# New prices in the builder's account of time: products and powers in the first block, passages between engines in the second

## The chip, the cores and the metric

The kernel runs on one core of a Trainium2 chip. The metric is the device time of one execution in microseconds (us); the times are medians of several runs. The profile is of one execution, with the time of each instruction on each engine: TensorE (PE, with its weight loads PEld), VectorE (DVE), ScalarE (ACT), GpSimd (POOL) and SyncE (SP, which issues the loads).

## What is computed

A row of 256 tokens of width 1024 goes through two blocks, in float32. The first block has two layers. Each norms its input, multiplies it with `w_in`, and mixes the tokens in three ways: retention (6 heads), dilated causal attention (6 heads) and a gated mixing within chunks of 128 tokens. The result goes through `w_out`, is normed and added; then comes a hidden layer of 2816 units.

```
for l in range(DEPTH):
    x = hybrid_layer(x, cos, sin, g_mix_pre[l], g_mix_post[l], w_in[l], w_s[l], b_s[l], w_out[l],
                     g_ffn_pre[l], g_ffn_post[l], w_gate_up[l], w_down[l])
```

The second block has an even layer (a Fourier mixing and attention with compressed keys, over the tokens and over 256 further context tokens) and an odd one (attention in a window with 16 heads, and to the context). Both take shifts, scales and gates from a vector times `w_mod`, the modulation. At the end `x` is normed.

## The kernel before

**Products.** Every weight is loaded as float32 in pieces of up to 128 x 1024 and split into a high part `whi` (by ACT) and a low part `wlo` (by DVE, a few by POOL). The activations are split the same way, into `xh` and `xl`. A product is then three passes of TensorE: high by high, high by low, low by high (`mm3`, and `mmT` with the weights held still). Their results stand in PSUM tiles: `mm` for input and hidden products, `sc` for scores and the sums of the mixing output and of the hidden layer, `tr` (two of them) for transpositions, small products and the modulation, and in the second block `s` for scores and outputs of attention.

**Order of the work.** TensorE's instructions run in the order in which the builder writes them; on the other engines the tile framework orders the work, with priorities that the builder gives. So the builder decides what TensorE does while ACT and DVE work on a head. It keeps an account of time for that, the class `Flow`: `now` is TensorE's time, `chain` the time at which the task in hand has its last result. `mm` and `transpose` (lines 366 to 381) add the cost of an instruction to `now`. `Lane.call` gives each instruction of ACT, DVE and POOL a cost (`Lane.cost`, line 281) and books it on its engine's lane in `Flow.op` (line 143); the next step of the task can start a latency `LAT` later. `from_pe` starts a chain one latency after TensorE's last product.

The tasks are generators: `rope` heads to turn, `dilated_task`, `retain_task`, `gmlp_task`, `y_att_task`, `y_ret_task`, the `Edge` between two parts of a layer (a norm of the sums: `rpost` and `rpre` are powers -0.5 on POOL, then `yn` is transposed), `modnorm_task`, and in the second block `unit`, `values`, `pair` and `mixed` for the heads. Each yields where it has to wait. A heap holds it with the time at which the account says that it can go on; `pump` runs up to three that are due after each triple of the big products. Where the big products themselves must wait (`wait`, `until`), the tasks that come due are run, and in a gap of 0.6 us or more `fill_gap` runs a piece of the modulation.

The lines that decide this:

```
def op(self, lane, cost):
...
    self.chain = t + cost + LAT
...
def pump(self, n=3):
    c = self.chain
    while n and self.heap and self.heap[0][0] + MARGIN <= self.now:
        self.run(heapq.heappop(self.heap)[2])
        n -= 1
    self.chain = c
...
if self.name == "pool":
    return 0.06 + n * (0.3e-3 if op == "memset" else 2.0e-3)
```

**Modulation.** `mod_step` (line 873) takes one to three loaded tiles of `w_mod` and multiplies each with 32 columns of the vector in four products that lie beside each other in TensorE's columns, in plain float32 (two instructions each in the trace). `mod_until` calls it at fixed places, `mod_spare` in gaps; in all there are 48 tiles. The next tile is loaded on SP's queue, where the weight loads are too.

**Loads and splits.** `load_ahead` issues the next weight load when the account has a raw buffer free, `fill` splits what has come, up to 4 us ahead of `now`, into a ring of eight pairs of tiles in the first block and five in the second.

The first block ends at line 1574, where its pools are closed; then the second begins. In the profile the first block's mixing lies at about 30 to 190 and 360 to 525 us, its hidden layers at 195 to 355 and 525 to 700 us, the even layer at 700 to 960 and the odd one at 960 to 1125 us.

Of the kernel before, what the change touches and what calls it, by code (L numbers as in the profile page):

```python
# [12 lines left out]
F32R = mybir.dt.float32r  # L13
# [3 lines left out]
OP = mybir.AluOpType  # L17
# [94 lines left out]
class Ev:  # L112


    def __init__(self):
        self.t = None
        self.waiters = []


LAT = 0.22  # L120
TR = "tr"
GAP = 0.6
MARGIN = 0.0
# [2 lines left out]
class Flow:  # L126
# [5 lines left out]
    def __init__(self):  # L132
        self.now = 0.0
        self.chain = 0.0
        self.heap = []
        self.n = 0
        self.lanes = {}
        self.tr = [0.0, 0.0]
        self.mm = [0.0, 0.0]
        self.marks = []  # L140
        self.spare = None

    def op(self, lane, cost):
        busy = self.lanes.setdefault(lane, [])
        while busy and busy[0][1] < min(self.now, self.chain) - 20.0:
            busy.pop(0)
        t = self.chain
        i = 0
        for i, (s, e) in enumerate(busy):
            if s - t >= cost:  # L150
                break
            t = max(t, e)
        else:
            i = len(busy)
        busy.insert(i, (t, t + cost))
        self.chain = t + cost + LAT


    def mark(self):
# [80 lines left out]

    def from_pe(self):

        self.chain = self.now + LAT

    def take_mm(self):
        self.mm.sort()
# [13 lines left out]
class Lane:  # L260
# [22 lines left out]
    def cost(self, op, n, kw):  # L283
        if self.name == "act":
            c = 0.06 + n * 0.833e-3
            if kw.get("accum_out") is not None:
                c += 0.1
            return c + (0.13 if n > 16 and kw.get("bias") is not None else 0.0)
        if self.name == "pool":
            return 0.06 + n * (0.3e-3 if op == "memset" else 2.0e-3)  # L290
        if op == "tensor_copy":
            return 0.08 + n * 0.8e-3
        return 0.07 + n * 1.04e-3
# [32 lines left out]
def block_kernel(ctx: ExitStack, tc: tile.TileContext, A, out, stop=None):  # L326
    nc = tc.nc
    pe = nc.tensor
    F = Flow()
# [3 lines left out]
    def pool(name, bufs=1, stack=ctx, **kw):  # L333
        return stack.enter_context(tc.tile_pool(name=name, bufs=bufs, reuse_waits="tile", **kw))
# [21 lines left out]
    def mmtile():  # L356
        F.take_mm()
        return pm.tile([P, 512], F32, name="mm")

    def trtile(dt=F32):  # L360
        F.take_tr()
        return pt.tile([P, 512], dt, name="tr")
# [5 lines left out]
    def mm(o, lhsT, rhs, start, stop_, cost=None, **kw):  # L368
        n = 1
        for s in o.shape[1:]:  # L370
            n *= s
        pe.matmul(o, lhsT, rhs, start=start, stop=stop_, **kw)  # L372
        if cost is None:
            cost = max(0.107, n * 0.417e-3 + 0.003) if lhsT.dtype == F32R else 2 * max(0.107, n * 0.833e-3 + 0.003)
        F.now += cost
        F.chain = max(F.chain, F.now + LAT)

    def transpose(o, i, idt):
        pe.transpose(o, i, idt)  # L379
        F.now += 0.056 if i.dtype == F32R else 0.108  # L380
        F.chain = max(F.chain, F.now + LAT)

    b1 = ExitStack()
    ps = pool("ps", 1, stack=b1, space=PSUM)
# [95 lines left out]
    for l in range(DEPTH):  # L480
        for i, key in enumerate(INP[l]):
            cc, n = PARTS[key]
# [87 lines left out]
    def load_mod():  # L570

        while cnt["mload"] < 48 and cnt["mload"] - cnt["mdone"] < RMOD:
            i = cnt["mload"]
            cnt["mload"] += 1
            raw = rmod[0].tile([P, D], F32, name="rawm")
            nc.sync.dma_start(raw, A["w_mod_2"][i // 24, i % 8 * P:i % 8 * P + P, i // 8 % 3 * D:i // 8 % 3 * D + D])
            F.chain = mod_t.pop(0)
            F.op("dma", 1024 * 1.6e-3)
            mraw.append((raw, F.chain + 2.0))
# [110 lines left out]
    def to_split(tr, gains, xh, xl):  # L690

        F.from_pe()
        for j, g in enumerate(gains):
            act.activation(xh[:, j], tr[:, j * P:(j + 1) * P], AF.Copy, scale=g)
            F.chain -= LAT
        F.chain += LAT
        for j, g in enumerate(gains):
            r = dve.scalar_tensor_tensor(xl[:, j], tr[:, j * P:(j + 1) * P], g, xh[:, j].bitcast(F32),
                                         op0=OP.mult, op1=OP.subtract)
            F.chain -= LAT  # L700
        F.chain += LAT
        return r

    def to_place(src, ks, xt, gains=None):
# [146 lines left out]
    def mslot(g):  # L851
        return 2 + g // 3 if g % 3 == 2 else g % 3
# [22 lines left out]
    def mod_step():  # L875

        i = cnt["mdone"]
        g, k = i // 8, i % 8
        F.until(mraw[0][1])
        n = 1  # L880
        while n < min(len(mraw), 8 - k) and mraw[n][1] <= F.now:
            n += 1
        raws = [mraw.pop(0)[0] for _ in range(n)]
        tr = trtile()
        for j in range(4):
            for a in range(n):
                mm(tr[32 * j:32 * j + 32, :256], mlh[:, k + a], raws[a][:, j * 256:(j + 1) * 256],
                   a == 0, a == n - 1, cost=0.429 if j == 0 else 0.027, tile_position=(0, 32 * j))
        mod_t.extend([F.now] * n)
        F.from_pe()  # L890
        if k == 0 and g % 3 == 2:
            dve.tensor_tensor(macc[:, mslot(g)], tr[:, :256], gbias[:, g // 3], op=OP.add)
        elif k == 0:
            dve.tensor_copy(macc[:, mslot(g)], tr[:, :256])
        else:
            dve.tensor_tensor(macc[:, mslot(g)], tr[:, :256], macc[:, mslot(g)], op=OP.add)
        F.free_tr()
        cnt["mdone"] += n
        load_mod()
        k += n - 1  # L900
        if k == 7 and g % 3 == 2:
            for j in range(4):
                nc.scalar.dma_start(gates[g // 3, :, j * 256:(j + 1) * 256], macc[32 * j:32 * j + 2, mslot(g)])
        if k == 7 and g % 3 == 1:
            F.spawn(mod_cols_task(g // 3))
# [199 lines left out]
    for l in range(DEPTH):  # L1105
# [391 lines left out]
        def up_T(c, w):  # L1497

            hbs = []
            zs = [mmtile(), mmtile()]  # L1500
            for a in range(2):
                for q in range(2):
                    for j in range(2):
                        for k in range(4 * q, 4 * q + 4):
                            mmT(zs[j][:, a * 256:(a + 1) * 256], w[8 * a + k], P * j, XH[fa][:, k], XL[fa][:, k],
                                k == 0, k == 7)
                            if k % 2:
                                F.pump()
                    done()
            F.from_pe()  # L1510
            for j in range(2):
                z = zs[j]
                F.chain = F.now + LAT
                with tc.high_priority(offset=HP):
                    h_ = act_h(z[:, 0:256], z[:, 256:512], "ptd%d" % j)
                    hb = hidden(2 * c + j)
                    act.activation(hb[:, 0], h_, AF.Copy)
                    dve.tensor_tensor(hb[:, 1], h_, hb[:, 0].bitcast(F32), op=OP.subtract)
                hbs.append(hb)
            for t in range(2):  # L1520
                h_ev[c, t] = Ev()
                hts[c, t] = [tuple(hb[:, i, t * P:(t + 1) * P] for i in range(2)) for hb in hbs]
                F.set(h_ev[c, t])
# [49 lines left out]
            return  # L1573
    b1.close()
    wpool[0] = rpool[0] = None
    w2 = pool("w2", 3)

    def work(name):
# [125 lines left out]
    def even_pass(b):  # L1704
# [270 lines left out]
        def fourier_task():  # L1975
            yield u_ev[0]
            yield u_ev[1]
            for g in range(4):
                yield TR
                tr = trtile()  # L1980
                for a in range(2):
                    mm(tr[:, :258], us[a][:, g * P:(g + 1) * P], dft[:, a * 258:(a + 1) * 258], a == 0, a == 1)
                t3 = tr[:, :258].rearrange("p (s n) -> p s n", s=2)
                aa = work("aa").rearrange("p (s n) -> p s n", s=2)
                act.activation(aa[:, :, 0:128], t3[:, :, 0:128], AF.Copy)
                F.chain -= LAT
                act.activation(aa[:, 0, 128:256], t3[:, 0, 128:0:-1], AF.Copy)
                F.chain -= LAT
                act.activation(aa[:, 1, 128:256], t3[:, 1, 128:0:-1], AF.Copy, scale=-1.0)
                F.free_tr()  # L1990
                yield TR
                tr = trtile()
                mm(tr[:, :256], cds[:, 0:P], aa[:, 0], True, False)
                mm(tr[:, :256], cds[:, P:2 * P], aa[:, 1], False, True)
                act.activation(yf[:, g], tr[:, :256], AF.Copy)
                F.free_tr()
            F.set(yf_ev)
# [123 lines left out]
    def evac_okv(t, z):  # L2121
# [6 lines left out]
            return v[:, :, None, :].to_broadcast([P, 4, 2, 64])  # L2128

        act.activation(vs[:, t], z4, AF.Copy, scale=0.5)  # L2130
        F.chain -= LAT
        if t < 2:
            act.activation(k4, both(src), AF.Copy)
            F.free_mm()
# [205 lines left out]
```

## Time and profile before

| what | value |
|---|---|
| median of 3 runs | 1134.96 us (1131.59, 1134.96, 1136.84) |
| the profiled execution's own time | 1136.02 us |
| its span, first to last instruction | 1134.2 us |
| TensorE busy | 1078.7 us, 95% of the span, 7066 products |
| DVE, ACT, POOL busy | 690.9, 580.5, 82.2 us |
| mean granted clock of TensorE | 0.984 |
| moved by DMA | 186.2 MB |

The span is a little shorter than the time of the execution, since that holds the start and end too. Busy time of TensorE counts an instruction from its start to its modelled end; products overlap in its pipeline, so the mean of one is longer than the distance from one start to the next. Most lines of the profile are those of helpers: L280 is the call of an ACT, DVE or POOL instruction, L372 a product, L379 a transposition; the tile names tell them apart. A wait is idle time of an engine just before an instruction, with the instruction that ended it.

### The profile page before, as it was taken

Reading aid. Unit: us, or ns where it says so; the run is one execution under the profiler, and the core shown is the slowest. Engines: PE = TensorE matmul, PEld = TensorE weight load, DVE = VectorE, ACT = ScalarE, POOL = GpSimd, SP = SyncE. Lnnn points to the kernel's source line nnn. Section 1 sums busy time; section 2 is a strip of 40 time slices with the busy share of each in tenths; the row PEclk is TensorE's granted clock in tenths of the full one; section 3 lists DMA queues with packets and bytes.
Section 4 is the critical chain, followed back from the end, with each engine's and each line's share of the span. In section 5 each row is a group of like instructions: output and inputs, shape, how many; then the busy total and the mean of one; then the engine's idle time right before and its main releaser. Section 6 shows DMA issues by size and latency. Waiting matters only on the chain.

```text
span 1134.2 us, 18304 instructions
## 1 busy us (share of the span) xinstructions
PE 1078.7 (95%) x7066; PEld 924.8 (82%) x7066; DVE 690.9 (61%) x1305; ACT 580.5 (51%) x1080; POOL 82.2 (7%) x98
## 2 busy tenths in 40 slices
PE   6899999999999999989999999899999999999996
PEld 4799778989888889768899898788977788767764
DVE  6766666555556766666755555653676547685653
ACT  5554464434344554456444443755655654555752
POOL 5120200000001120200000001000000000000000
PEclk9999999999999999999999999899999999999999
DMA  8654468666764745477666652651453325442300
GB/s 269 208 186 149 147 206 262 198 218 195 237 207 152 240 124 195 132 255 248 211 194 185 212 156 73 203 166 43 135 184 116 91 77 181 135 134 94 112 2 37
DMA packets 115991, 186.20 MB, mean 164 GB/s; under 512 B 6939, under 2 KB 84104, under 8 KB 115904
## 3 DMA queue, kind: packets, MB, share of 16 engines
q1 hardware_dynamic: 112896, 179.33, 50.0%
q10 hardware_dynamic: 2512, 5.44, 1.4%
q8 instruction: 55, 0.90, 0.3%
q0 software_dynamic: 496, 0.27, 0.1%
q14 instruction: 32, 0.26, 0.1%
HBM read 183.95 MB, written 1.06 MB: 163 GB/s over the span
## 4 chain that ended last, share of the span: by engine, by line
PE 80%; DVE 7%; ACT 4%; issue 4%; DMA 3%; POOL 1%; ACTq 0%; DVEq 0%; POOLq 0%
PE mm L372 49%; PE sc L372 16%; PE s L372 6%; PE tr L379 5%; PE tr L372 5%; DVE wlo L280 3%; ACT whi L280 1%; DVE xl L280 1%; DMA raw<-in_w_in_dram 1%; DMA raw<-in_o_w_in_dram 1%; ACT xh L280 1%; DMA nsink<-in_o_sink_dram 1%; ACT dump L280 0%; POOL rkv L280 0%; DMA first<-in_g_mix_pre_dram 0%
## 5 line engine op out<-in xcount | busy, mean ns | idle before, releaser
L280 DVE TENSOR_TENSOR wlo<-raw,whi 128x1024 fp32r<-128x1024 f32 (+4 forms) x311 | 352.1, 1139 | 201.8 <-ACT whi L280 198.7
L280 ACT ACTIVATE whi<-raw 128x1024 fp32r<-128x1024 f32 (+4 forms) x313 | 301.6, 974 | 235.9 <-PE mm L372 148.6
L372 PE MATMUL mm<-xh,whi 128*128 128x256 f32 x768 | 225.5, 294 | 0.0
L372 PE MATMUL mm<-whi,xh 128*128 128x384 f32 (+2 forms) x564 | 217.7, 386 | 4.1 <-ACT whi L280 2.9
L372 PE MATMUL mm<-xh,wlo 128*128 128x256 f32 x768 | 217.6, 283 | 0.0
L372 PE MATMUL mm<-xl,whi 128*128 128x256 f32 x768 | 217.6, 283 | 0.0
L372 PE MATMUL mm<-wlo,xh 128*128 128x384 f32 (+2 forms) x564 | 207.9, 369 | 4.7 <-DVE wlo L280 2.4
L372 PE MATMUL mm<-whi,xl 128*128 128x384 f32 (+2 forms) x564 | 207.3, 368 | 1.7 <-DVE xl L280 1.7
L372 PEld LDWEIGHTS mm<-xh,whi 128*128 128x128 f32 x768 | 147.2, 192 | 8.3 <-issue 7.1
L372 PEld LDWEIGHTS mm<-xh,wlo 128*128 128x128 f32 x768 | 147.4, 192 | 0.9
L372 PEld LDWEIGHTS mm<-xl,whi 128*128 128x128 f32 x768 | 147.4, 192 | 0.0
L372 PEld LDWEIGHTS mm<-whi,xh 128*128 128x128 f32 x564 | 108.7, 193 | 23.8 <-issue 6.7
L372 PEld LDWEIGHTS mm<-wlo,xh 128*128 128x128 f32 x564 | 109.0, 193 | 16.3 <-DVE wlo L280 4.9
L372 PEld LDWEIGHTS mm<-whi,xl 128*128 128x128 f32 x564 | 108.6, 192 | 14.0 <-DVE xl L280 2.4
L372 PE MATMUL sc<-whi,fhs 128*128 128x512 f32 x352 | 114.8, 398 | 0.0
L372 PEld LDWEIGHTS sc<-whi,fhs 128*128 128x128 f32 x352 | 66.2, 188 | 18.0 <-issue 2.1
L372 PE MATMUL sc<-wlo,fhs 128*128 128x512 f32 x176 | 69.6, 395 | 0.0
L280 ACT ACTIVATE pp<-tr 128x512 f32<-128x512 f32 x56 | 32.9, 593 | 29.7 <-PE tr L379 29.5
L372 PE MATMUL tr<-rawm,mlh 128*32 128x256 f32 x384 | 41.0, 384 | 0.0
L372 PEld LDWEIGHTS sc<-wlo,fhs 128*128 128x128 f32 x176 | 33.1, 188 | 7.0
L280 POOL TENSOR_TENSOR rpost<-pe,mhalf 128x1 f32<-128x1 f32 x8 | 4.3, 541 | 422.9 <-DVE pe L280 422.9
L372 PEld LDWEIGHTS tr<-rawm,mlh 128*32 128x32 f32 x384 | 20.9, 109 | 15.4 <-issue 1.4
(341 smaller groups left out, 1354.8 us busy)
## 6 DMA issues: line engine op xcount, KB each, us to landing
raw<-in_w_gate_up_dram SPq DMA_DIRECT2D x72, 512.0 KB, 4.5
rawm<-in_w_mod_dram SPq DMA_DIRECT2D x48, 512.0 KB, 6.0
raw<-in_w_down_dram SPq DMA_DIRECT2D x44, 512.0 KB, 4.2
raw<-in_w_in_dram SPq DMA_DIRECT2D x56, 384.0 KB, 3.7
raw<-in_e_w_in_dram SPq DMA_DIRECT2D x24, 512.0 KB, 4.8
raw<-in_o_w_in_dram SPq DMA_DIRECT2D x20, 512.0 KB, 3.9
raw<-in_w_out_dram SPq DMA_DIRECT2D x16, 512.0 KB, 4.7
raw<-in_w_gate_up_dram SPq DMA_DIRECT2D x32, 256.0 KB, 4.4
```

The lines of the kernel that those rows point to most:

```text
L280: return fn(*args, **kw)
L372: pe.matmul(o, lhsT, rhs, start=start, stop=stop_, **kw)
L379: pe.transpose(o, i, idt)
```

## The change

The latency and two prices become fields of the account. In the first block a product of split numbers costs 0.014 us beside its columns (before: 0.003), a power on POOL 0.35 us and 0.155 for each column (before: 0.06 and 0.002), and each product of a modulation tile 0.217 (before: 0.429 for the first of four, 0.027 for the others); the latency stays 0.22. At the beginning of the second block the first two go back to the old prices, and the latency becomes 0.32. No instruction of the program is added or removed by an edit; the account is used while the program is built, and not on the chip.

```
-LAT = 0.22
...
+        self.lat = 0.22
+
+        self.over = 0.014
+        self.powers = True
...
-        self.chain = t + cost + LAT
+        self.chain = t + cost + self.lat
...
-        self.chain = self.now + LAT
+        self.chain = self.now + self.lat
...
         if self.name == "pool":
+            if kw.get("op") == OP.pow and self.f.powers:
+                return 0.35 + n * 0.155
             return 0.06 + n * (0.3e-3 if op == "memset" else 2.0e-3)
...
         if cost is None:
-            cost = max(0.107, n * 0.417e-3 + 0.003) if lhsT.dtype == F32R else 2 * max(0.107, n * 0.833e-3 + 0.003)
+            cost = max(0.107, n * 0.417e-3 + F.over) if lhsT.dtype == F32R else 2 * max(0.107, n * 0.833e-3 + 0.003)
         F.now += cost
-        F.chain = max(F.chain, F.now + LAT)
+        F.chain = max(F.chain, F.now + F.lat)
...
                 mm(tr[32 * j:32 * j + 32, :256], mlh[:, k + a], raws[a][:, j * 256:(j + 1) * 256],
-                   a == 0, a == n - 1, cost=0.429 if j == 0 else 0.027, tile_position=(0, 32 * j))
+                   a == 0, a == n - 1, cost=0.217, tile_position=(0, 32 * j))
...
     b1.close()
     wpool[0] = rpool[0] = None
+
+    F.over, F.powers, F.lat = 0.003, False, 0.32
     w2 = pool("w2", 3)
```

The other lines of the diff put `F.lat` in the place of `LAT` (in `transpose`, `to_split`, `up_T`, `fourier_task` and `evac_okv`).

## Rows read from the trace of the kernel before

**Rows 1.** The page: its first line and TensorE's busy time.
```profile
span 1134.2 us, 18304 instructions
...
PE 1078.7 (95%) x7066; PEld 924.8 (82%) x7066; DVE 690.9 (61%) x1305; ACT 580.5 (51%) x1080; POOL 82.2 (7%) x98
```

**Rows 2.** Stretches: length, busy PE, PEld, DVE, ACT, POOL, clock, DMA share, GB/s.
```profile
30.00:195.00 165.00, 158.62 (x946) 138.63 (x947) 111.68 (x225) 86.96 (x164) 24.37 (x26) 0.98 0.60 194
195.00:355.00 160.00, 160.00 (x1123) 143.60 (x1122) 84.41 (x119) 67.31 (x98) 1.08 (x2) 1.00 0.64 202
355.00:525.00 170.00, 160.26 (x936) 136.57 (x935) 114.61 (x233) 89.68 (x175) 28.34 (x26) 0.98 0.57 186
525.00:695.00 170.00, 168.76 (x1190) 153.67 (x1189) 98.79 (x146) 72.18 (x101) 0.54 (x1) 1.00 0.61 191
695.00:845.00 150.00, 141.29 (x978) 124.70 (x976) 88.17 (x169) 90.06 (x201) 8.12 (x11) 0.98 0.46 140
...
960.00:1085.00 125.00, 119.62 (x798) 95.59 (x798) 85.95 (x208) 74.96 (x150) 1.04 (x2) 0.97 0.37 115
```

**Rows 3.** Chain that ended last, hidden layer: start, length, what, how many.
```profile
190.60 5.59 PE sc L372 x24
196.20 11.50 PE mm L372 x96
...
241.88 2.80 PE tr L372 x24
```

**Rows 4.** TensorE's waits, 30 to 700 us: total us, times, longest.
```profile
PE tr L379 <- DVE xl L280: 8.0, 5, 3.4
PE tr L379 <- POOL ropeq L280: 2.9, 1, 2.9
PE tr L379 <- DVE y L280: 1.9, 1, 1.9
PE tr L379 <- ACT yn L280: 1.8, 2, 0.9
PE mm L372 <- DVE xl L280: 1.3, 1, 1.3
PE tr L379 <- DVE cx L280: 1.2, 1, 1.2
PE tr L379 <- ACT ptd L280: 0.8, 1, 0.8
PE tr L372 <- ACT ptd L280: 0.3, 1, 0.3
```

**Rows 5.** TensorE's waits, 720 to 1120 us, those within tasks: total, times, longest.
```profile
PE s L372 <- ACT pp L280: 2.8, 4, 0.9
PE tr L379 <- DVE oq L280: 2.5, 1, 2.5
PE s L372 <- DVE oat L280: 2.0, 1, 2.0
...
PE tr L379 <- ACT qa L280: 1.1, 1, 1.1
...
PE tr L379 <- ACT kn L280: 0.7, 1, 0.7
PE tr L379 <- DVE qtT L280: 0.7, 1, 0.7
...
PE tr L379 <- DVE kvt L280: 0.5, 1, 0.5
```

**Rows 6.** Powers on POOL, grouped by shape: busy us, mean ns | idle before.
```profile
L280 POOL TENSOR_TENSOR rrr<-rre,mhalf 128x4 f32<-128x4 f32 x6 | 8.0, 1327 | 48.7 <-DVE rre L280 48.7
...
L280 POOL TENSOR_TENSOR rpost<-pe,mhalf 128x1 f32<-128x1 f32 x8 | 4.3, 541 | 422.9 <-DVE pe L280 422.9
```

**Rows 7.** TensorE in order of time at two edges; in brackets the idle time.
```profile
141.74 0.33 PE L379 MATMUL tr<-c,yn 128*128 128x128 f32 x1 [0.92 <-ACT yn L280]
...
507.52 0.44 PE L379 MATMUL tr<-c,fh 128*128 128x128 f32 x2 [3.36 <-DVE xl L280]
```

More of the change, by code (lines that the diff above doesn't have):

```diff
@@ L380, in transpose @@
         F.now += 0.056 if i.dtype == F32R else 0.108
-        F.chain = max(F.chain, F.now + LAT)
+        F.chain = max(F.chain, F.now + F.lat)
     b1 = ExitStack()
@@ L694, in to_split @@
             act.activation(xh[:, j], tr[:, j * P:(j + 1) * P], AF.Copy, scale=g)
-            F.chain -= LAT
-        F.chain += LAT
+            F.chain -= F.lat
+        F.chain += F.lat
         for j, g in enumerate(gains):
@@ L699, in to_split @@
                                          op0=OP.mult, op1=OP.subtract)
-            F.chain -= LAT
-        F.chain += LAT
+            F.chain -= F.lat
+        F.chain += F.lat
         return r
@@ L1512, in up_T @@
                 z = zs[j]
-                F.chain = F.now + LAT
+                F.chain = F.now + F.lat
                 with tc.high_priority(offset=HP):
@@ L1985, in fourier_task @@
                 act.activation(aa[:, :, 0:128], t3[:, :, 0:128], AF.Copy)
-                F.chain -= LAT
+                F.chain -= F.lat
                 act.activation(aa[:, 0, 128:256], t3[:, 0, 128:0:-1], AF.Copy)
-                F.chain -= LAT
+                F.chain -= F.lat
                 act.activation(aa[:, 1, 128:256], t3[:, 1, 128:0:-1], AF.Copy, scale=-1.0)
@@ L2130, in evac_okv @@
         act.activation(vs[:, t], z4, AF.Copy, scale=0.5)
-        F.chain -= LAT
+        F.chain -= F.lat
         if t < 2:
```

## The prediction

> **What bounds the kernel now.** I read the page's span and busy times first: TensorE is busy 1078.7 of 1134.2 us [rows 1], so the time is TensorE's work plus what it stands idle. The table by stage says where [rows 2]: in the two stretches of hidden-layer products (195 to 355 and 525 to 695 us) it has no more than 1.2 us to lose; in the two mixing stretches of the first block (30 to 195, 355 to 525) it lacks 6.4 and 9.7 us, in the second block 8.7 (695 to 845) and 5.4 (960 to 1085). The change removes no product and no transfer. It alters only the account of time by which the builder decides after which product a waiting task (a transposition, a small product) is put into TensorE's order. TensorE runs that order as written, so a task put in too early is an idle TensorE, and one put in too late costs only if something at the end of a stage waits for it.
>
> What such mistakes cost now stands in the lists of TensorE's waits: 18.2 us in 13 waits in the first block after its start [rows 4], and 10.3 us in the waits of the second that the account could move [rows 5]. That is the ground the change plays on: 28.5 us, 2.5% of the time.
>
> **Does the account err as the change supposes?** The chain of waits has a pure run of 96 products of 256 columns in 11.50 us, 0.1198 each, and 24 of 512 columns in 5.59 us, 0.233 each [rows 3]. The account before holds 256 x 0.000417 + 0.003 = 0.110 and 0.2165; the change makes it 0.121 and 0.2275. A piece of the modulation is three weight tiles in 2.80 us, 0.93 a tile [rows 3], where the account has 0.429 + 3 x 0.027 = 0.51 and after the change 4 x 0.217 = 0.87. POOL's power takes 0.54 us for one column and 1.0 and more for four [rows 6]; the account has 0.062 and 0.068, after the change 0.505 and 0.97. So in the first block all three new prices lie nearer to the rows. In the second block prices stay as they are and each passage from engine to engine is counted 0.10 longer.
>
> [...]
>
> **The change part by part, in the profiled execution's 1136.0 us (span 1134.2 and 1.8 around it).**
>
> *Products, first block.* A wait of W us in the account is covered by W / 0.110 products, which really last 1.09 W. After the change it is covered by W / 0.121, 0.99 W. So a tenth of the cover goes: of a wait of some 3 us (the ACT and DVE steps between two products of a task; an estimate: a handful of steps as long as those in [rows 6], 0.5 to 1.3 us) about 0.27 us. A task that already stalls is put in 0.27 us earlier and stalls that much more. 13 waits stall; three of them are cured by the next part, and two by filling (both below), so eight pay: 8 x 0.27 = +2.2. Lower bound 0 (a task that comes earlier also ends its stage's chain earlier); upper bound, every task step of the block, by the code about 39 a layer (8 turned heads, 9 of the dilated attention, 3 of retention, 3 of the gating, 4 of y, 8 at the edges, 4 of the hidden layer): 78 x 0.27 = +21. I take +2.2, near the lower end, because the list shows 13 stalls only among these 78 [rows 4].
>
> *Powers, first block.* At an edge the order is rpost, rpre, then the transpositions of yn: two powers, each counted 0.54 - 0.06 = 0.48 too short [rows 6], 0.96 together. TensorE stalls there 0.92 us, twice (one of them in [rows 7], the sum of 1.8 in [rows 4]). Counted rightly, the transposition goes in behind one or two more triples of 512 columns, of which there are many at that place, and both stalls go: -1.8. In front of the last mixing products the transposition of y stalls 1.9 us [rows 4] behind retention's power of four columns, counted 1.0 - 0.07 = 0.9 too short: -1.0 of it. Together -2.8; bounds 0 and, if the y stall goes whole, -3.7.
>
> *Modulation, first block.* Its 48 tiles must run somewhere; the account puts them into gaps of 0.6 us or more. The edges lose 1.3 (a product waiting for xl [rows 4]) and 3.4 us (the transposition of fh [rows 7]), where the account, too short by the powers, saw less of a gap. With a longer gap and the true price one tile of 0.93 us goes into each of two edges: -1.9. Bounds: 0, and -4.7, both stalls whole. A tile that moves takes its next load along on SP, ahead of or behind weight loads; I cost this at nothing, because in the hidden layer, where most tiles run, TensorE is busy 160.00 of 160.00 us [rows 2] with such loads among its weights; without that cover one late load would show as a wait of a few us.
>
> *Weight splits.* As the account's products last longer, the splits of coming weights into high and low parts come earlier among the tasks on ACT and DVE. No wait for a split stands among the first block's [rows 4], so nothing is to be gained, and a split put ahead of a task's step can cost that step's wait, at most about the 1.3 us that the product waits for xl now; I leave it at 0 and keep the 1.3 for the range.
>
> *Latency, second block.* No row shows the account's passages, so I go by the steps in each chain that ends in a stall. The waits for pp have two passages (TensorE to ACT, ACT to TensorE): four waits x 0.2. oq has three, 0.3; oat, from the scores through the soft maximum to the output, about eight, 0.8; qa four, 0.4; kn three, 0.3; qtT and kvt four each, 0.8 together. Sum -3.4 out of 10.3 us that these stall (2.8 + 2.5 + 2.0 + 1.1 + 0.7 + 0.7 + 0.5 [rows 5]). Waits on the main line itself gain nothing, since the builder has no other task to put there. Bounds: -10.3, and +4.8 if the later tasks run out of cover: in the last layer 16 pairs go through three chains, 5.3 in each, with about nine passages a pair, 5.3 x 9 x 0.1 = 4.8 us later by the account. I take -3.4: the stage from 960 to 1085 us still has 119.6 of 125 us of work in it [rows 2], so cover is there.
>
> **The sum:** 1136.0 + 2.2 - 2.8 - 1.9 - 3.4 = 1130.1. The profiled execution lies 1.1 over the median of the runs (1136.02 against 1134.96), so 1129.0 against 1134.96: 0.53% faster. About 0.5%, 5.7 us, is what a measurement can tell from no change, since three runs of one kernel spread over 5.3 us.
>
> **The rivals.**
> 1. *The stalls move, and nothing is won.* Each task that comes at another place pushes its neighbours; two buffers for transpositions serve all tasks, and a stall cured at one is found at the next (the five transpositions that wait for xl, 8.0 us, wait for such a buffer [rows 4]). Then the gains of 8.1 and the loss of 2.2 come out even: 1136.0 - 1.1 = 1134.9, or 1133 with a part of them. For it speaks that no price touches those 8.0 us directly; against, that the yn stalls match the mispriced powers to 0.04 us. 0.16.
> 2. *Slack was what held the first block together: slower.* Place: the task steps of the two mixing stretches. Price 0.27 us a step. It decides once the typical slack of a step is under 0.27 us; if two thirds of the 78 steps pay, 52 x 0.27 = 14 us, and 1136.0 + 14 - 2.8 - 3.4 - 1.1 = 1142.7. For it: latency in that block stays 0.22, so nothing replaces the slack, and the change itself lengthens it in the other block. Against: only 13 of the steps stall now. [...] 0.24.
> 3. *More is won than summed:* the fillable stalls of the second block go whole (-10.3) and the edges too (-4.7), with the powers -2.8 and no loss of slack: 1136.0 - 17.8 - 1.1 = 1117. Against: a tenth of a us a passage is small beside stalls of 2 us. 0.06, counted as faster.
> 4. *The change does not do what it says:* the order stays nearly the same, since tasks are put in only after whole triples of products (0.36 to 0.7 us), coarser than many corrections: 1134 to 1136. Against: 0.27 us on a wait is near half a triple, so about every other task would move. 0.04, counted as no change.
>
> **How the numbers follow.** The forecast has 0.50. Its own range is 1120 (powers -3.7, filling -4.7, the latency's term twice, no loss: 1119.7) to 1134 (powers and loss alone: 1134.3); the bound of 0.5%, 1129.3, cuts it, and since most of its terms have more room below than above, 0.36 of it counts as faster and 0.14 as no change. With rival 3 faster has 0.42; with rivals 1 and 4 no change has 0.34; slower is rival 2's 0.24. The point is the forecast's own, 1129.0. The range for 8 in 10 reaches from rival 3 (1117, with a us for the runs' spread: 1116) to rival 2 with a split's 1.3 us (1144); what it leaves out is most of rival 2's far end (78 steps, 1150) and larger gains.
>
> **What would show it.** Right: the two yn waits of 0.92 us gone, the y wait near 1.0, the hidden layer's stretches unchanged at no idle, waits of the second block down by some 3 us, most in oq, oat and pp; TensorE's products as many and as long as before. Wrong: more than 13 waits, or over 20 us, between 30 and 700 us; new waits for ropeq, pd or ptd in the mixing stretches (rival 2); or the same sum of waits under other names (rival 1). If the last stretch after 1085 us is longer than before, the added latency ran out of cover.

## The result and the profile after

The changed kernel takes 1120.92 us (median of 6 runs, 1116.10 to 1121.85) against 1134.84 us (6 runs): ratio 0.9875, 95% interval 0.9857 to 0.9893. It is 13.9 us faster, more than twice the 5.9 us forecast. The sign was right, the size was not.

The page of the changed kernel begins with span and busy times; they answer to [rows 1].

```profile
span 1119.5 us, 18293 instructions
...
PE 1070.4 (96%) x7066; PEld 920.3 (82%) x7066; DVE 688.7 (62%) x1304; ACT 579.7 (52%) x1080; POOL 83.7 (7%) x98
```

TensorE runs the same 7066 products. It stands idle 49.1 us in place of 55.5, 6.4 less; but its busy time also fell, by 8.3 us, although no product went. The clock says why. The table by stage (length, busy time and count on PE, PEld, DVE, ACT and POOL, granted clock, share of DMA, GB/s) has it beside the busy time and answers to [rows 2].

```profile
30.00:195.00 165.00, 157.89 (x951) 139.76 (x952) 115.15 (x228) 88.39 (x166) 24.95 (x26) 0.99 0.60 188
195.00:355.00 160.00, 160.00 (x1123) 142.20 (x1122) 83.45 (x119) 66.26 (x97) 1.08 (x2) 1.00 0.67 209
355.00:525.00 170.00, 162.64 (x978) 142.58 (x977) 118.23 (x237) 93.91 (x179) 27.31 (x26) 0.99 0.59 193
525.00:695.00 170.00, 170.00 (x1181) 152.37 (x1181) 95.89 (x147) 70.90 (x102) 1.08 (x2) 1.00 0.60 187
695.00:845.00 150.00, 143.00 (x992) 125.65 (x991) 92.31 (x172) 91.20 (x202) 8.72 (x10) 0.98 0.49 150
...
960.00:1085.00 125.00, 120.18 (x863) 94.67 (x863) 83.26 (x209) 76.35 (x159) 1.05 (x1) 1.00 0.30 95
```

From 960 to 1085 us the clock is 1.00 where it was 0.97, from 355 to 525 us 0.99 for 0.98. Over the whole span the mean granted clock is 0.990 after and 0.984 before, so the time lost to it, estimated as (1 - clock) x span, is about 0.010 x 1119.5 = 11.2 us after and 0.016 x 1134.2 = 18.1 us before: 6.9 us gained. The lists of waits between 30 and 1120 us sum to 29.1 us after and 35.2 before: 6.1 us gained. Together that is 13.0 of the 14.7 us between the spans. Of the rest, 0.3 us is idle time outside the lists (6.4 - 6.1) and 1.4 us busy time beyond the clock (8.3 - 6.9).

These are two single executions, and the one of before had one of the lowest clocks of its kind. The 48 executions of the kernel before that were timed beside the experiments have a mean clock of 0.987 (0.983 to 0.992), which is 15.1 us lost; the six of the changed kernel have 0.990, 11.4 us lost. Over the runs the clock thus gives about 3.7 us of the 13.9, not half of it.

TensorE's waits in the changed kernel, 30 to 700 us (total, times, longest), answer to [rows 4]:

```profile
PE tr L384 <- DVE xl L283: 4.9, 3, 3.6
PE tr L384 <- POOL ropeq L283: 3.7, 2, 2.5
PE mm L377 <- DVE fh L283: 2.5, 1, 2.5
PE tr L384 <- ACT yn L283: 2.1, 2, 1.2
PE mm L377 <- DVE xl L283: 1.3, 1, 1.3
PE tr L384 <- DVE macc L283: 0.2, 1, 0.2
PE tr L384 <- ACT Tq L283: 0.2, 1, 0.2
```

They sum to 14.9 us in 11 waits, where there were 18.2 in 13. The y wait (1.9) and the cx wait (1.2) are gone, xl lost two of its five; yn is not cured (2.1 against 1.8), and a wait for fh is new. Some of it moved: the longest wait for xl is now 3.6 us, in front of a transposition of ropeq, where the kernel before waits 1.2. In the second block (720 to 1120 us), for [rows 5]:

```profile
PE s L377 <- ACT pp L283: 4.2, 8, 0.8
PE tr L384 <- ACT kn L283: 1.9, 1, 1.9
PE s L377 <- DVE rt L283: 1.1, 1, 1.1
...
PE s L377 <- DVE oat L283: 0.6, 1, 0.6
```

The wait for oq (2.5) is gone altogether and oat fell from 2.0 to 0.6. The waits for pp grew from four to eight, of at most 0.8 us each, and kn from 0.7 to 1.9: in the main long waits went and short ones came.

One edge shows what a changed order does. Before, at the edge of the second layer, the eight transpositions of yn came right behind the modulation; they took both transposition buffers, and the first pair of fh had to wait 3.36 us until ACT and DVE had emptied one [rows 7 has the end of it]. TensorE in order of time before:

```profile
500.13 2.87 PE L372 MATMUL tr<-rawm,mlh 128*32 128x256 f32 x24
502.93 1.24 PE L379 MATMUL tr<-c,yn 128*128 128x128 f32 x8
```

and after:

```profile
494.96 1.09 PE L377 MATMUL tr<-rawm,mlh 128*32 128x256 f32 x16
495.99 0.44 PE L384 MATMUL tr<-c,fh 128*128 128x128 f32 x2
...
496.96 1.05 PE L384 MATMUL tr<-c,yn 128*128 128x128 f32 x8
```

In the account yn is ready later now, so fh and a triple of products go first, and nobody waits for the buffer. (With the new price of the powers alone, e5 below, TensorE has the same order there.) What follows the wait of 3.36 us before shows the second half of its price (columns as in the table by stage):

```profile
504.00:507.50 3.50, 0.17 (x2) 0.00 (x0) 1.93 (x8) 1.79 (x7) 0.00 (x0) 1.00 0.95 359
507.50:511.50 4.00, 3.98 (x13) 3.19 (x14) 0.76 (x3) 1.53 (x3) 0.00 (x0) 0.59 0.82 330
511.50:515.00 3.50, 3.50 (x16) 2.85 (x16) 0.87 (x3) 2.81 (x4) 0.54 (x1) 0.98 0.00 0
```

In the 4 us after the wait the granted clock is 0.59: products of 512 columns start 0.43 us apart there (508.28 to 509.56 us), and 0.23 us apart behind 511.68 us. By the clock 4.0 x 0.41 = 1.6 us are lost beside the 3.36, an estimate. After 511.5 us the clock is at 0.98. This second half is not paid every time. The kernel e2 below has the first block of the kernel before, in the same order, and the same wait; in its execution the clock behind it stayed at 1.00:

```profile
503.94 0.44 PE L384 MATMUL tr<-c,fh 128*128 128x128 f32 x2 [3.35 <-DVE xl L283]
...
503.90:507.90 4.00, 3.96 (x20) 3.28 (x21) 0.66 (x2) 1.49 (x3) 0.00 (x0) 1.00 0.83 335
```

Nor does it need a long wait. In the profiled execution of before, half clock (a granted clock of 0.50) also set in at the last of four waits of 0.2 to 0.8 us close together:

```profile
708.59 0.44 PE L372 MATMUL mm<-whi,xh 128*128 128x384 f32 x1 [0.66 <-ACT ka L280]
710.31 0.44 PE L372 MATMUL mm<-wlo,xh 128*128 128x384 f32 x1 [0.24 <-DVE pe L280]
712.23 0.45 PE L372 MATMUL mm<-whi,xh 128*128 128x384 f32 x1 [0.78 <-ACT whi L280]
713.22 0.69 PE L372 MATMUL mm<-wlo,xh 128*128 128x384 f32 x1 [0.55 <-DVE wlo L280]
...
713.00:716.40 3.40, 3.18 (x10) 3.18 (x11) 2.33 (x4) 1.98 (x4) 0.00 (x0) 0.50 0.69 202
```

### The profile page after: what moved, and what is told of

Read it like the earlier page. It is cut to its first block, busy times and chain, and to the rows that moved or that the text cites. A ratio compares the mean times of both kernels' runs of the same rounds, so it can differ in the third digit from the quotient of the medians.

```text
span 1119.5 us, 18293 instructions
## 1 busy us (share of the span) xinstructions
PE 1070.4 (96%) x7066; PEld 920.3 (82%) x7066; DVE 688.7 (62%) x1304; ACT 579.7 (52%) x1080; POOL 83.7 (7%) x98
## 4 chain that ended last, share of the span: by engine, by line
PE 77%; DVE 7%; ACT 6%; issue 4%; DMA 3%; POOL 2%; ACTq 0%; DVEq 0%; POOLq 0%
PE mm L377 47%; PE sc L377 16%; PE s L377 6%; PE tr L377 5%; PE tr L384 5%; DVE wlo L283 2%; ACT whi L283 2%; DVE xl L283 1%; DMA raw<-in_w_in_dram 1%; DMA nsink<-in_o_sink_dram 1%; ACT xh L283 1%; DVE junk L283 1%; ACT po L283 1%; DMA raw<-in_w_gate_up_dram 1%; DVE po L283 1%
## 5 line engine op out<-in xcount | busy, mean ns | idle before, releaser
L377 PE MATMUL mm<-whi,xh 128*128 128x384 f32 (+2 forms) x564 | 216.5, 384 | 4.4 <-ACT ka L283 2.5
L377 PEld LDWEIGHTS mm<-whi,xl 128*128 128x128 f32 x564 | 108.0, 191 | 13.9 <-DVE xl L283 2.7
L377 PEld LDWEIGHTS sc<-whi,fhs 128*128 128x128 f32 x352 | 66.1, 188 | 19.6 <-issue 2.9
```

## The experiments

All ratios are to the kernel before, timed on the same chip beside the run.

**The two blocks apart.** e1_first_block keeps the first block's part, e2_second_block the second's.

Against the changed kernel, e1 is

```
-    F.over, F.powers, F.lat = 0.003, False, 0.32
+    F.over, F.powers, F.lat = 0.003, False, 0.22
```

and e2

```
-        self.over = 0.014
-        self.powers = True
+        self.over = 0.003
+        self.powers = False
...
-                   a == 0, a == n - 1, cost=0.217, tile_position=(0, 32 * j))
+                   a == 0, a == n - 1, cost=0.429 if j == 0 else 0.027, tile_position=(0, 32 * j))
```

> The change in the first block alone; in the second the old prices and the old latency 0.22. Theory A (the gain is the stalls that go and the half-clock stretches that followed them, each part by itself): the changed kernel's lead at the border of the blocks, 7.2 us, remains and the second block is as before: 1134.8 - 7.2 = 1127.6, ratio 0.994. Rival B (the two parts act together, or one of them is the whole gain): 1121 to 1123 if the first block is all of it, 1134 to 1136 if it is none.

> The change in the second block alone: latency 0.32 there, all prices old. Theory A: no difference before the border, then the second block's 7.5 us: 1134.8 - 7.5 = 1127.3, ratio 0.993. Rival B: 1121 to 1123 if it is all, 1134 to 1136 if it is none. If e1 and e2 together gain clearly less or more than 14 us, the parts are not independent.

Measured: e1 1125.61 us, ratio 0.9922 (0.9904 to 0.9940); e2 1128.60 us, 0.9943 (0.9929 to 0.9958). The parts give 8.9 and 6.5 us, together 15.3 against the whole change's 14.2 by its ratio: the blocks are independent within the intervals. Both came out as theory A has it, and rival B falls. In e1, with the old latency, the second block's waits for oq (2.3) and oat (2.0) are still there:

```profile
PE tr L384 <- DVE oq L283: 2.3, 1, 2.3
PE s L377 <- DVE oat L283: 2.0, 1, 2.0
```

In e2, with the old prices and the latency of 0.32, oq is gone and oat is at 0.6. So it is the latency that takes them away.

**The first block's three prices, one at a time** (each on the old prices, latency 0.22 in both blocks): e3_products has `self.over = 0.014` alone, e4_modulation `cost=0.217` alone, e5_powers `self.powers = True` alone.

> In the first block only the price of the big products is new (0.014 beside the columns); modulation, powers and the second block as before. Theory C (the gain of the first block comes from modulation tiles that leave the edges, and they leave because the account's products last longer, so that it sees fewer gaps before weights and events): 1128 to 1130, and tiles between 460 and 530 us down from 56 instructions. Rival D (they leave because a tile itself is priced at 0.87 in place of 0.51): 1133 to 1136, tiles as before. The slack rival of the prediction (less cover, slower): 1137 to 1143.

> In the first block only the price of a modulation tile is new (four products at 0.217); products, powers and the second block as before. Theory D: 1128 to 1130, tiles between 460 and 530 us down from 56 instructions. Theory C: 1133 to 1136.

> In the first block only the price of POOL's powers is new; products, modulation and the second block as before. The prediction's term: -2.8 us, 1132.0, the two yn waits of 0.92 us gone. What the changed kernel's trace suggests (yn still stalls there, since weight splits on ACT and DVE hold the edge up and not the account's power): 1134 to 1136, both yn waits still at 0.9 or more.

Measured: e3 1132.40 us, 0.9976 (0.9956 to 0.9996); e4 1128.73 us, 0.9946 (0.9928 to 0.9964); e5 1121.24 us, 0.9891 (0.9871 to 0.9910). The gains are 2.7, 6.1 and 12.4 us by the ratios. (The runs of e3 spread from 1128.6 to 1141.0 us, and its trace is of the slowest.) Theory D has the time of e4 right, 1128 to 1130, and its fall in tiles; but the tiles do not make the gain: their instructions between 460 and 530 us, 56 before, are 44 in e3, 48 in e4 and 65 in e5, the fewest with the smallest gain and the most with the largest. And the three do not add up: alone they make 21 us, together (e1) 8.9. The powers alone gain nearly as much as the whole change does in both blocks. The waits of e5_powers from 30 to 700 us:

```profile
PE mm L377 <- DVE xl L283: 3.0, 3, 1.3
PE mm L377 <- ACT ka L283: 2.2, 1, 2.2
PE tr L384 <- POOL ropeq L283: 2.1, 1, 2.1
PE tr L384 <- DVE xl L283: 2.0, 2, 1.2
...
PE tr L384 <- DVE y L283: 0.8, 1, 0.8
...
PE tr L384 <- ACT yn L283: 0.5, 2, 0.2
```

Without ka, which already belongs to the second block, that is 10.3 us where there were 18.2. Here the prediction's own places are met: yn falls from 1.8 to 0.5, y from 1.9 to 0.8, and the transpositions that wait for xl from 8.0 to 2.0, the fh waits of 3.36 and 1.63 among those gone. The products' waits for xl grew from 1.3 to 3.0. The second expectation, drawn from the changed kernel's trace, that yn would stall all the same, was wrong.

**What a stall costs.** e8 and e9 put four stalls into the hidden layers of the changed kernel, where TensorE never idles (busy 160.00 of 160.00 and 170.00 of 170.00 us). Both have the same TensorE instructions; e9's chain has four POOL additions more, the `tensor_tensor` line four times. e9's lines:

```
+            if c in (4, 8):
+                tp = pt.tile([P, 512], F32, name="tr")
+                pe.transpose(tp[:, 0:P], ident, ident)
+                wb = b1p.tile([P, 512], F32, name="wb")
+                with tc.high_priority(offset=HP):
+                    nc.scalar.activation(wb[:, 0:P], tp[:, 0:P], AF.Copy)
+                    nc.gpsimd.tensor_tensor(wb[:, 0:P], wb[:, 0:P], ident, op=OP.add)
...
+                pe.transpose(tp[:, P:2 * P], wb[:, 0:P], ident)
```

> The changed kernel with four stalls put into the hidden layers, where TensorE never idles (chunks 4 and 8 of both layers): a transposition of the identity, its copy by ACT, and a transposition of the copy, whose results nobody reads. Each stall about 0.8 us. Theory A (a short stall costs its length, a long one its length and a half-clock stretch of 3.4 us, 1.7 us of work): 1120.9 + 4 x (0.8 + 0.3 for the two transpositions) = 1125.3, clock of 195 to 355 and 530 to 690 us still 1.00. Rival E (the stalls' own length is all there is, short or long): the same here.

> As e8_short_stalls, with four additions on POOL between the copy and the second transposition, so that each stall lasts about 2.5 us; TensorE's instructions are the same. Theory A: four half-clock stretches more than in e8_short_stalls, 1125.3 + 4 x 1.7 (longer stalls) + 4 x 1.7 (clock) = 1138.9. Rival E: 1132.1, and no more half-clock stretches than before.

Measured: e8 1125.38 us, 0.9933 (0.9917 to 0.9948); e9 1148.51 us, 1.0128 (1.0110 to 1.0146). The stalls were longer than planned in both; in e9 the first POOL addition of each chain took 1.33 us. Who waited for the tile wb, in e8:

```profile
  PE tr L1512: 5.0, 4
```

and in e9:

```profile
  PE tr L1516: 17.0, 4
```

So four stalls of 1.25 us and four of 4.25. e8's stalls cost 4.5 us over the changed kernel by the medians and 6.6 by the ratios, for 5.0 us of waits and eight added transpositions: about their own length. The clock is 1.00 over both stretches of hidden layers (195 to 355 and 525 to 695 us), as in the 6 us behind the first stall:

```profile
207.50:213.50 6.00, 5.90 (x49) 5.91 (x50) 2.36 (x2) 1.10 (x2) 0.00 (x0) 1.00 0.60 175
```

e9 costs 23.1 us more than e8, of which the stalls' length is 17.0 - 5.0 = 12.0. The other 11.1 are in the products behind them. The table by stage of e9, the first stall and what follows it, then the stretches behind the other three:

```profile
208.00:212.40 4.40, 0.19 (x2) 0.00 (x0) 2.27 (x2) 1.22 (x2) 2.69 (x4) 0.90 0.57 156
212.40:215.40 3.00, 2.95 (x14) 2.96 (x15) 0.00 (x0) 0.00 (x0) 0.00 (x0) 0.50 0.46 152
215.40:218.40 3.00, 3.00 (x16) 3.00 (x15) 0.00 (x0) 0.27 (x1) 0.00 (x0) 0.51 0.00 0
218.40:221.40 3.00, 3.00 (x27) 3.00 (x26) 1.23 (x1) 1.01 (x2) 0.00 (x0) 1.00 0.00 0
...
294.50:300.90 6.40, 5.60 (x30) 5.60 (x30) 0.35 (x2) 0.00 (x0) 0.67 (x2) 0.55 0.32 99
...
567.50:573.00 5.50, 4.96 (x23) 4.96 (x24) 0.00 (x0) 0.00 (x0) 0.46 (x1) 0.50 0.35 105
...
648.00:653.00 5.00, 5.00 (x32) 5.00 (x32) 0.52 (x3) 0.34 (x1) 0.00 (x0) 0.66 0.18 66
```

In 3 us at a clock of 0.50 there are 14 to 16 products, at 1.00 there are 27. A product of 256 columns starts 0.213 us after the one before it in place of 0.120:

```profile
216.13 0.41 PE L377 MATMUL mm<-xh,wlo 128*128 128x256 f32 x1
216.35 0.41 PE L377 MATMUL mm<-xl,whi 128*128 128x256 f32 x1
...
218.78 0.28 PE L377 MATMUL mm<-xh,whi 128*128 128x256 f32 x1
218.90 0.28 PE L377 MATMUL mm<-xh,wlo 128*128 128x256 f32 x1
```

By the starts of the products, half clock lasts 5.8, 5.0, 5.2 and 3.4 us behind the ends of the four stalls, 19.4 us in all, of which 1 - 0.120 / 0.213 = 0.44 is lost: 8.5 us. Between the two profiled executions (1146.41 and 1124.74 us) the excess is 21.7 - 12.0 = 9.7 us, between the medians 11.1. So a stall of 4.25 us costs 2.1 to 2.8 us more than its length, where theory A had 1.7. With the stalls at their measured length rival E gives 1125.4 + 12.0 = 1137.4 us, and 1148.5 were measured: rival E falls, and theory A holds for these two lengths. Lengths between them were not tested by themselves.

**Latency and prices in other places.** e6_long_first is the changed kernel with `self.lat = 0.32` from the start; e7_all_prices keeps the new prices in the second block (`F.lat = 0.32` alone there); e10_powers_long has old prices but for the powers in the first block and 0.32 in both, e11_powers_then_long the same with 0.22 in the first; e12_old_prices_long has all prices old and 0.32 in both.

> The changed kernel with latency 0.32 in the first block too. If the new product price had taken slack that the first block needs (the prediction's slower rival), the longer latency gives it back: 1115 to 1118. If slack is not what stalls it: 1119 to 1123. If tasks put in later lengthen the mixing chains: 1124 or more.

> The changed kernel, but the second block keeps the new prices of products and powers, beside its latency of 0.32. If the new product price takes cover that tasks need (theory F, cover: too early is what costs), 2 to 5 us slower than the changed kernel: 1123 to 1126. If prices nearer to the measured ones are better by themselves (theory G): 1117 to 1119. No difference (1119 to 1123): the second block is insensitive to both.

> Old prices of products and modulation everywhere, POOL's powers priced as measured in the first block, latency 0.32 in both blocks. Theory F: the first block as in e5_powers or better (-12 to -14 us), the second as in e2_second_block (-6.5): 1114 to 1116, the fastest kernel. Theory G (the products' price is worth its gain): slower than e6_long_first, 1118 to 1124.

> e5_powers with the second block's latency at 0.32: old prices of products and modulation, powers as measured in the first block, latency 0.22 in the first and 0.32 in the second. If the blocks are independent, as e1_first_block and e2_second_block say: -11.9 - 6.5, 1116 to 1117. If the gain of e5_powers was partly in how it entered the second block: 1119 or more.

> All prices as before, only the latency 0.32 in both blocks. Theory F in its plain form (any added cover does, powers are one way to add it): first block better than before by 4 us or more on top of the second's 6.5: 1121 to 1124. If the powers had to be priced rightly: 1127 to 1130, as e2_second_block.

| kernel | us | ratio, interval |
|---|---|---|
| e6_long_first | 1116.44 | 0.9846 (0.9829 to 0.9862) |
| e7_all_prices | 1125.11 | 0.9921 (0.9900 to 0.9941) |
| e10_powers_long | 1122.07 | 0.9895 (0.9872 to 0.9918) |
| e11_powers_then_long | 1117.61 | 0.9861 (0.9836 to 0.9887) |
| e12_old_prices_long | 1129.91 | 0.9967 (0.9950 to 0.9984) |

e7 against the changed kernel: the new prices cost the second block 0.0046, 5 us, and the intervals lie just apart, a reason to keep the old prices there. It fits the loss of cover that the prediction's slower rival spoke of, but does not show it: the prices of products and of powers were not changed apart there. Its trace has one long new wait for a buffer:

```profile
718.89 0.48 PE L384 MATMUL tr<-c,kp 128*128 128x128 f32 x1 [3.60 <-DVE kvt L283]
```

e11, with the old price of products, gains 15.8 us by its ratio, where the two blocks apart sum to 12.4 + 6.5 = 18.9: the blocks are nearly independent here too (1116 to 1117 us expected, 1117.6 measured). The ranges that go with cover (theory F) were met in e6 and e7 and missed in e10 (1114 to 1116) and e12 (1121 to 1124), so it does not hold as a rule: more latency in the first block probably helps with the new prices (e6), but not with the powers alone (e10 against e11) nor with the old prices (e12 against e2). e12 keeps the fh wait (3.4 us for xl in its list), since yn still comes first at the edge; e10 gets a wait of 2.59 us for the context rows that e11 does not have. Each variant has an order of its own, and the lists suggest, without showing it, that one or two long waits make much of the differences. e6 has the lowest ratio of all; its interval and the changed kernel's just touch (0.9862 and 0.9857), so its lead of some 3 us is likely, not certain.

## Why the prediction was right and wrong

**The step that failed is the first one:** "the time is TensorE's work plus what it stands idle", and with it every term of the sum, which priced a stall at its own length. e9 shows that a stall of 4.25 us takes 2.1 to 2.8 us more with it, in products at half clock, and the trace of before has a clock of 0.59 over 4 us behind the fh wait, an estimated 1.6 us. The clock stood in [rows 2], 0.98 and 0.97 in just the stretches where TensorE stands idle 5.4 us or more and 1.00 in the others, and no term of the sum uses it. A second step failed beside it: the +2.2 us that the longer price of products was to cost, which no run bears out: alone that price gained 2.7 us (e3).

How much each is worth, against the kernel before: the waits by the lists from 30 to 1120 us (one execution each), the clock by (1 - mean granted clock) x span over all runs of a kernel, which overstates it somewhat, since products at half clock lose 0.44 of their time and not 0.5.

| kernel | waits, us | clock, us | sum | measured by the ratio |
|---|---|---|---|---|
| changed kernel | 6.1 | 3.7 | 9.8 | 14.2 |
| e1_first_block | 5.3 | 2.5 | 7.8 | 8.9 |
| e2_second_block | 0.9 | 2.6 | 3.5 | 6.5 |
| e5_powers | 6.9 | 4.1 | 11.0 | 12.4 |
| e6_long_first | 11.2 | 4.9 | 16.1 | 17.5 |

The forecast of 5.9 us is near the 6.1 of the waits; the clock is what it left out, and 1 to 4 us a row stay unexplained. The lists are no finer than about 2 us: the first block is the same in before and e2 (18.2 and 19.6 us of waits) and in the changed kernel and e1 (14.9 and 12.7). That the whole of the waits came out as forecast is partly luck, since the single terms did not:

- *Products, +2.2.* Alone -2.7 (e3): wrong in sign. (By its own figures, 1.09 and 0.99 of 3 us, a step is 0.30 us and not 0.27, the term +2.4.) Beside the other new prices the sign may be right, which is not shown: e1, which is e5 with the new prices of products and modulation added, is 0.0031 slower than e5, but these intervals overlap, and e7 loses 5 us in the other block, with the price of the powers changed too.
- *Powers, -2.8.* The place was right, the edges, and the yn and y waits fell in e5 nearly as written (1.8 to 0.5, 1.9 to 0.8). The term was 12.4 alone. What was missed is the clock, and that a later yn also lets the first fh go ahead, so that the waits for a transposition buffer go (8.0 to 2.0 us): the prediction's first rival had said that no price touches those. In the whole change yn stalls again (2.1 us).
- *Modulation, -1.9.* Alone -6.1 (e4), and not by filling: tiles between 460 and 530 us became fewer, from 56 instructions to 48 in e4 and to 42 in the changed kernel. The expected filling of this edge did not happen; where the 6.1 us come from is not shown.
- *Loads at nothing.* Right: the hidden layers have no idle time at all after the change (160.00 of 160.00 and 170.00 of 170.00).
- *Latency, -3.4.* 6.5 measured (e2). oat lost 1.4 us and oq all of its 2.5, not 0.8 and 0.3: a task goes behind a whole triple or not at all, so a correction of tenths can move a wait by its whole length. pp, from which 0.8 was expected, grew from 2.8 to 4.3. The clock of the stage from 960 to 1085 us rose from 0.97 to 1.00, but that is not the latency's alone: in e1, with both waits still there, it was 0.99.
- *Rival 1* (stalls only move) is refuted by the time and the sums of waits, 35.2 to 29.1, though the 3.6 us for xl did move. *Rival 2* (slack) did not decide; its sign, more waiting for ropeq, was seen in part (2.9 to 3.7 us), and e7 fits its mechanism, without showing it. *Rival 3*, at 1117, came nearest, by waits that did not go whole and a clock that it did not count. *Rival 4* is refuted by the order at the edge.
- *The price of a product.* Products of 512 columns follow one another at 233 ns in the trace [rows 3], where the account before has 216.5 and the changed one 227.5 in the first block. Whether the account should hold the measured price is another question, and e11 against the changed kernel says that this kernel does not need it.

**What stays open:** which order a given set of prices leads to. The gains of single prices do not add up in the first block (21 us alone, 8.9 together), and no rule on cover that was tried told all of e6, e10 and e12. Open too is when a wait of a length between e8's 1.25 us and e9's 4.25 us is followed by half clock, and when not: the wait of 3.4 us for fh was followed by it in before (0.59 over 4 us) and not in e2 (1.00).

## What to carry to other kernels

Price a stall of TensorE with what comes behind it, in e9 2.1 to 2.8 us more than a stall's own 4.25 us: look at the granted clock in the stretch after each long wait, and count the products there that run at half speed (in e9 0.213 us from start to start in place of 0.120). Look at the clock of several executions before you put a figure on it: one profile against another gave 6.9 us here, the runs 3.7. A long wait taken away can be worth more than its length (behind before's 3.36 us stood an estimated 1.6 us more); whether one cut into short ones is, no run here tests, and in before half clock set in at four short ones of 0.2 to 0.8 us close together too (0.50 over 3.4 us). A model that orders the work acts by thresholds: test each of its constants alone and together, since a correction of a tenth of a microsecond can move whole tasks, and the gains of constants that help alone need not add up.

## What the runs showed of the hardware that was not expected

Behind the four stalls of 1.25 us TensorE's clock stayed at 1.00; behind each of the four of 4.25 us came 3.4 to 5.8 us at half clock (0.50 and 0.51 behind the first), in which a product of 256 columns took 0.213 us in place of 0.120. A wait of 3.4 us in one and the same order was followed by half clock in one execution (0.59 over 4 us) and by 1.00 in another. Of e9's POOL additions the first took 1.33 us and the three after it 0.45 each; in the first chain the first ran beside a split of weights on DVE (209.26 to 210.49 us) and the others beside none, and no run here separates that from its being the first.
